# Second layer's heads of a fused three-block model: the split exponentials are transposed by DMA instead of by TensorE

## The chip, the cores and the metric

The kernel runs on one core of one Trainium2 chip, in one launch. The metric is the device time of the whole launch in microseconds, the median of three runs. A change of some 0.5% can be told from none.

## The reference, cut to what matters

The program computes two layers of a first model (a differential and top-k attention layer, then a latent attention layer), and then a second model (a Fourier and windowed attention block with sixteen experts). The change lies in the second layer, the latent attention with 16 heads over 1024 tokens:

```python
def mla_attention(q_nope, q_rope, k_nope, k_rope, v):     # 16 heads, 64 + 32 dims, v 64
    def block(args):                                      # one block of 128 queries
        s = (jnp.einsum('bqhd,bkhd->bhqk', qn, k_nope)
             + jnp.einsum('bqhr,bkr->bhqk', qr, k_rope)).astype(jnp.float32) * scale
        s = jnp.where(chunk_mask(qpos, kpos), s, -jnp.inf)   # causal in chunks of 64
        p = jax.nn.softmax(s, axis=-1)
        return jnp.einsum('bhqk,bkhd->bqhd', p.astype(v.dtype), v)
    ...
def mla_layer(x, ...):
    ...
    o = mla_attention(q_nope, q_rope, k_nope, k_rope, v).reshape(b, s_len, C_WIDTH)
    return x + (o * jax.nn.silu(gate)) @ w_o
```

## The kernel before, in words

Everything is float32 at the interface. A float32 product is made of three TensorE products of high and low parts (`mm3`, L137 to L141). `layer1` (L1034) first projects and stores the latents, then runs a loop over 16 heads (from L1207). A head loads its q and k parts from device memory over SyncE's queue into two-deep buffers (L852, L1212 to L1220), and every fourth head loads v for four heads (L1223).

A head has eight blocks of 128 queries. Since the mask is causal, block qb has qb + 1 blocks of keys. The blocks are packed into five packs, `PACK1` = (7), (6, 0), (5, 1), (4, 2), (3), so a pack has 8, 8, 8, 8 and 4 blocks of 128x128. For each pack (L1229): TensorE makes the scores in PSUM banks (L293), VectorE takes the row maximum and writes masked scores to the SBUF tile `e` (L317, three buffers), VectorE makes the bias `nm` (L1245), ScalarE takes the exponentials in place with their sums (L1247), and `p_to_T` (L331) turns `e` around: TensorE transposes up to four blocks into a PSUM bank `ptp` (L340), ScalarE casts the bank to float16 `pTh` (L341), VectorE subtracts that cast from the bank and writes the rest as float16 `pTl` (L342). `pv_mm` then multiplies with v, three products for each block: `pTh` with both parts of v (L350, L351) and `pTl` with the high part (L352). `norm_o` (L794, the product L801) takes the head's result out, and every second head stores it (L1265).

Between packs the loop runs units of other work: gate products (L783 to L785) in the first eight heads, totals of a modulation vector (L1309 to L1320, each with loads, one small product and a store) from the sixth head on, the second model's bias rows, the output weights (L915 to L919) and halves of the output product (L944 to L949, L1001 to L1011) later. The order of all instructions on each engine, SyncE's queue included, is fixed ahead of the run by a planner that lists the program by its own estimate of each instruction's time. An engine takes its instructions in that order and waits at the head of it. Nearly all loads and stores of this stage go through SyncE's queue.

Two other stages use `p_to_T` too: the first layer's heads (L672, L714) and the second model's windowed attention (L1576).

Of the kernel before, what the change touches and what calls it, by code (L numbers as in the profile page):

```python
# [11 lines left out]
F32 = mybir.dt.float32  # L12
F32R = mybir.dt.float32r
F16 = mybir.dt.float16
# [3 lines left out]
ALU = mybir.AluOpType  # L18
# [4 lines left out]
P = 128  # L23
S = 1024
D = 1024
NT = S // P
# [269 lines left out]
def score_banks(kk, parts, pairs):  # L296


    bs = [kk.bank() for _ in range(0, parts[-1][2], 512)]
    r = []  # L300
    for qb, c0, c1 in parts:
        ps = []
        for b in range(c0 // 512, (c1 - 1) // 512 + 1):
            x0, x1 = max(c0, 512 * b), min(c1, 512 * b + 512)
            sc = bs[b][:, x0 - 512 * b:x1 - 512 * b]
            score_mm(kk, sc, pairs(qb), x0 - c0, x1 - x0)
            ps.append((sc, x0 - c0, x1 - c0))
        r.append(ps)
    return r


def row_max(kk, e, segs, mx):

    last = -3.0e38
    for i, (sc, term, x0, x1) in enumerate(segs):
        m = mx if i == len(segs) - 1 else kk.sm([P, 1], tag="rmx")
        kk.nc.vector.tensor_tensor_reduce(e[:, x0:x1], sc, kk.zeros.to_broadcast([P, x1 - x0]) if term is None else term, scale=1.0, scalar=last,  # L317
                                          op0=ALU.add, op1=ALU.max, accum_out=m)
        last = m


def offsets(pack):

    r, c = [], 0
    for qb in pack:
        r.append((qb, c, c + (qb + 1) * P))
        c += (qb + 1) * P
    return r


def p_to_T(kk, ps, pool, p, nb, cap=NT):  # L331

    nc = kk.nc
    hi = pool.tile([P, cap, P], F16, tag="pT_h", name=kk.nm("pTh"))
    lo = pool.tile([P, cap, P], F16, tag="pT_l", name=kk.nm("pTl"))
    for g in range(0, nb, 4):
        w = min(4, nb - g)
        pt = ps.tile([P, 4, P], F32, tag="tr", name=kk.nm("ptp"))
        for j in range(w):
            nc.tensor.transpose(pt[:, j, :], p[:, (g + j) * P:(g + j + 1) * P], kk.ident)  # L340
        nc.scalar.copy(hi[:, g:g + w, :], pt[:, :w, :])  # L341
        nc.vector.tensor_tensor(lo[:, g:g + w, :], pt[:, :w, :], hi[:, g:g + w, :], op=ALU.subtract)  # L342
    return hi, lo


def pv_mm(kk, out, hi, lo, v1, v2, nb, off=0):

    mm = kk.nc.tensor.matmul
    for j in range(nb):
        mm(out, hi[:, j, :], v1(off + j), start=j == 0, stop=False)  # L350
        mm(out, hi[:, j, :], v2(off + j), start=False, stop=False)  # L351
        mm(out, lo[:, j, :], v1(off + j), start=False, stop=j == nb - 1)  # L352
# [120 lines left out]
def layer0(kk, ps, a, hT, mix_d, gate_d, wo, mod):  # L473
# [145 lines left out]
    for h in range(4):  # L619
# [27 lines left out]
        for i, pack in enumerate(PACK0):  # L647
# [21 lines left out]
            for z, (qb, c0, c1) in enumerate(parts):  # L669
                both = nc.vector.scalar_tensor_tensor(es[0][:, c0:c1], es[1][:, c0:c1], ra[:, z:z + 1], es[0][:, c0:c1],  # L670
                                                      op0=ALU.mult, op1=ALU.add).ins
            hi, lo = p_to_T(kk, ps, pp, es[0], n // P)  # L672
            if i == 0 or at + w > 4:
                pv, at = kk.pv(P), 0
# [119 lines left out]
def norm_o(kk, o, pv, st, vsc):  # L794

    nc = kk.nc
    rs = kk.sm([P, NT], tag="brs")
    nc.vector.reciprocal(rs, st)
    r2 = kk.sm([P, NT], tag="brs2")
    nc.vector.tensor_scalar(r2, rs, vsc[:, 1:2], None, op0=ALU.mult)  # L800
    nc.vector.tensor_tensor(o, pv, r2[:, :, None].to_broadcast([P, NT, 64]), op=ALU.mult)  # L801
# [46 lines left out]
def load_stack(kk, pool, src, row0, tag, lo_first=False, into=None, cols=slice(0, S)):  # L848

    t = pool.tile([P, cols.stop - cols.start], F32R, tag=tag, name=kk.nm(tag), bufs=2) if into is None else into  # L850
    for z in range(2):
        kk.nc.sync.dma_start(t[64 * z:64 * z + 64, :].bitcast(F32), src[z ^ int(lo_first)][row0:row0 + 64, cols])  # L852
    return t
# [180 lines left out]
def layer1(kk, ps, a, hT, hold, mix_d, gate_d, wo, mod, wx):  # L1034

    nc = kk.nc
# [154 lines left out]
    ap_ = ax.enter_context(kk.pool(name="at2", bufs=2))  # L1191
# [15 lines left out]
    for h in range(16):  # L1207
        r0 = 64 * h
        q1 = load_stack(kk, None, qn_d, r0, "q1", into=kp[:, 3 + h % 2, :])
        k1 = kp[:, 5 + h % 2, :]  # L1210
        for z in range(2):
            nc.sync.dma_start(k1[64 * z:64 * z + 64, :].bitcast(F32), kn_d[0][r0:r0 + 64, :])  # L1212
        q2 = ap_.tile([P, S], F32R, tag="q2", name=kk.nm("q2"))
        nc.sync.dma_start(q2[0:64, :].bitcast(F32), qn_d[0][r0:r0 + 64, :])
        for i in range(2):
            for z in range(2):
                b = 64 + 32 * i + 16 * z
                nc.sync.dma_start(q2[b:b + 16, :].bitcast(F32), qr_d[z][i][16 * h:16 * h + 16, :])
        k2 = kp[:, h % 2, :]
        at_ = nc.sync.dma_start(k2[0:64, :].bitcast(F32), kn_d[1][r0:r0 + 64, :]).ins  # L1220
        if h % 4 == 0:
            with kk.tc.issue_after(lk[-1]) if h else ExitStack():
                nc.sync.dma_start(vh[:, :, :, r0:r0 + 256], v_d[:, :, :, r0:r0 + 256])  # L1223
        lk.append(at_)
        if h % 2 == 0:
            o = ap_.tile([P, NT, P], F32, tag="o", name=kk.nm("oc"), bufs=1)
        st = kk.sm([P, NT], tag="bst")
        pv = kk.pv(64)
        for i, pack in enumerate(PACK1):  # L1229
            parts = offsets(pack)  # L1230
            n = parts[-1][2]
            e = ap_.tile([P, S], F32, tag="p", name=kk.nm("e"), bufs=3)
            mx = kk.sm([P, 2], tag="mxc")
            nm = kk.sm([P, 2], tag="nmx")

            def pairs(qb):
                sl = slice(qb * P, (qb + 1) * P)
                return (q1[:, sl], k1), (q2[:, sl], k2), (q2[:, sl], k3)

            rows_ = score_banks(kk, parts, pairs)  # L1240
            for z, (qb, c0, c1) in enumerate(parts):
                d = S - (c1 - c0)
                row_max(kk, e[:, c0:c1], [(sc, hide[:, d + x0:d + x1], x0, x1) for sc, x0, x1 in rows_[z]], mx[:, z:z + 1])
            z = len(pack)
            nc.vector.tensor_scalar(nm[:, 0:z], mx[:, 0:z], -CS, LN_PSC, op0=ALU.mult, op1=ALU.add)  # L1245
            for z, (qb, c0, c1) in enumerate(parts):
                nc.scalar.activation(e[:, c0:c1], e[:, c0:c1], AF.Exp, bias=nm[:, z:z + 1], scale=CS, accum_out=st[:, qb:qb + 1])  # L1247
            hi, lo = p_to_T(kk, ps, ap_, e, n // P)
            for qb, c0, c1 in parts:
                b = slice(c0 // P, c1 // P)  # L1250
                pv_mm(kk, pv[:, qb, :], hi[:, b], lo[:, b], lambda j: vh[:, j, 0, r0:r0 + 64], lambda j: vh[:, j, 1, r0:r0 + 64],
                      qb + 1)
            if h >= 5 and i % 2 == 0:
                mod2.run(1, mp)
            if (h, i) in BIAS1_AT:
                rows.run(1, mp)
            if h < GATES1_HEADS and i in (1, 3):
                gates.run(1)
            if h == GATES1_HEADS and i < 4 or h >= 12 and i == 0:
                prep.run(1)  # L1260
            if (h, i) in HALF1_AT:
                halves.run(1)
        norm_o(kk, o[:, :, (h % 2) * 64:(h % 2) * 64 + 64], pv, st, vsc)
        if h % 2:
            nc.sync.dma_start(mix_d[:, (h // 2) * P:(h // 2 + 1) * P].rearrange("(t p) c -> p t c", p=P), o)  # L1265
        if h == GATES1_HEADS - 1:
            gates.run()
            gx.close()
            lhs_pool = wx.enter_context(kk.pool(name="lhs1", bufs=1, side="right"))
            prep, halves = wo(hx.enter_context(kk.pool(name="wx1", bufs=1, side="right")), lhs_pool)  # L1270
# [602 lines left out]
def tile_model(ctx: ExitStack, tc: tile.TileContext, a: dict, out: bass.AP, part=None):  # L1873
# [61 lines left out]
    bias_d, rows = bias_rows(kk, ps, a["rel_bias_2"], a["c_oh2"], 8, 384, 33, "b2", 8.0, last=-BIG)  # L1935
    wx = ExitStack()
    layer1(kk, ps, a, hT1, hold, mix_d[1], gate_d[1], wo1, (totals, rows), wx)

    def finish_l1(op, hook):
# [229 lines left out]
```

## Time and profile before

| | us |
|---|---|
| runs, median of 3 | 2592.82 |
| lowest, highest | 2587.34, 2599.93 |
| the profiled execution, device time | 2589.32 |
| its span in the profile | 2587.5 |

The page of the profile gives the busy time of each engine over the span and the chain of work that ended last. Engines: PE is TensorE's products, PEld its loading of the stationary operand, DVE VectorE, ACT ScalarE, POOL GpSimd, SPq SyncE's queue of DMA issues. A line such as L340 is that of the kernel, and where a helper serves several stages, the stretch of time tells them apart. The heads of the second layer run from about 1090 to 1462 us of the span.

### The profile page before, as it was taken

The numbers are of one execution on the slowest core, as the hardware profiler recorded it, in microseconds if no ns is written. First come the engines' busy times: TensorE is split into PE (matmuls) and PEld (weight loads), VectorE is DVE, ScalarE is ACT, GpSimd is POOL, SyncE is SP. The second block draws the span as 40 slices with busy tenths as digits, with TensorE's granted clock in tenths as the row PEclk, the third lists the DMA queues.
The fourth block names the chain that finished last, engine by engine and source line by source line (L and its number), as shares of the span: only waits on it lengthen the run. The fifth ranks groups of instructions, "written<-read, shape, count | busy, mean of one in ns | idle before, by whom it ended". The sixth has DMA issues, their size and how long they took to land.

```text
span 2587.5 us, 40940 instructions
## 1 busy us (share of the span) xinstructions
PE 2355.9 (91%) x14412; PEld 1843.1 (71%) x14412; DVE 1797.5 (69%) x4575; ACT 1347.5 (52%) x2635; POOL 438.7 (17%) x626
## 2 busy tenths in 40 slices
PE   7988888898998878999989979989985999999998
PEld 6866666676777866788767768877864777777776
DVE  4459987877986355366776674677666777777775
ACT  4345675455653333255564375355452666666664
POOL 0000147757740013100000000011000101110110
PEclk9999888899999899999999989989997999999999
DMA  4442476566656227854776461545684999999994
GB/s 131 127 135 79 135 204 184 158 188 191 188 154 208 78 99 258 260 147 123 182 192 170 133 204 55 137 111 163 190 302 184 347 382 351 358 363 374 359 353 137
DMA packets 302637, 523.80 MB, mean 202 GB/s; under 512 B 46022, under 2 KB 191582, under 8 KB 302432
## 3 DMA queue, kind: packets, MB, share of 16 engines
q1 hardware_dynamic: 287456, 467.70, 55.5%
q0 software_dynamic: 14976, 53.49, 6.6%
q8 instruction: 114, 1.87, 0.3%
q14 instruction: 91, 0.75, 0.1%
HBM read 405.18 MB, written 115.65 MB: 201 GB/s over the span
## 4 chain that ended last, share of the span: by engine, by line
PE 61%; DMA 15%; DVE 10%; issue 4%; POOL 4%; ACT 4%; SPq 1%; POOLq 0%; DVEq 0%; ACTq 0%
PE sb L139 6%; PE sb L140 6%; PE sb L141 6%; PE sb L293 5%; PE ptp L340 3%; DMA adw<-w_ada 3%; PE w_gate L1815 2%; PE w_down L1815 2%; PE w_up L1815 2%; DVE tkj L397 2%; PE w_gate L139 2%; PE w_gate L141 2%; PE w_up L139 2%; PE w_up L141 2%; PE w_up L140 2%
## 5 line engine op out<-in xcount | busy, mean ns | idle before, releaser
L341 ACT CAST pTh<-ptp 128x512 f16<-128x512 f32 (+2 forms) x316 | 166.1, 557 | 134.8 <-PE ptp L340 129.0
L342 DVE TENSOR_TENSOR pTl<-ptp,pTh 128x512 f16<-128x512 f32 (+2 forms) x316 | 199.9, 648 | 38.1 <-ACT pTh L341 37.4
L1683 DVE TENSOR_TENSOR ring_l<-mraw,ring_h 128x1024 fp32r<-128x1024 f32 x152 | 183.8, 1223 | 33.6 <-ACT ring_h L1682 31.0
L340 PE MATMUL ptp<-ident,e 128*128 128x128 f32 x1184 | 182.2, 284 | 7.6 <-DVE e L670 2.1
L1682 ACT CAST ring_h<-mraw 128x1024 fp32r<-128x1024 f32 x152 | 156.4, 1048 | 59.0 <-PE w_up L141 20.8
L1683 DVE TENSOR_TENSOR ring_l<-xraw,ring_h 128x1024 fp32r<-128x1024 f32 x136 | 164.7, 1223 | 29.4 <-ACT ring_h L1682 27.0
L1682 ACT CAST ring_h<-xraw 128x1024 fp32r<-128x1024 f32 x136 | 140.7, 1049 | 46.2 <-PE w_up L141 19.9
L340 PEld LDWEIGHTS ptp<-ident,e 128*128 128x128 f32 x1184 | 133.4, 144 | 20.2 <-issue 4.0
L1247 ACT ACTIVATE e<-e,nmx 128x1024 f32<-128x1024 f32 (+7 forms) x128 | 98.4, 770 | 74.5 <-DVE nmx L1245 74.3
L352 PEld LDWEIGHTS <-pTl 128*128 128x128 f16 x1184 | 108.5, 99 | 35.6 <-issue 15.0
L350 PEld LDWEIGHTS <-pTh 128*128 128x128 f16 x1184 | 110.2, 100 | 30.9 <-issue 21.4
L1772 POOL DMA_INDIRECT xg<-h_d,idx x16 | 24.0, 1502 | 598.5 <-DVE gate L1775 550.7
L1298 POOL TENSOR_SCALAR adw<-adw,ada_s 128x256 f32<-128x256 f32 x192 | 109.1, 580 | 93.1 <-DMA adw<-w_ada 92.4
L902 ACT ACTIVATE e<-e,nmx 128x1024 f32<-128x1024 f32 (+7 forms) x128 | 98.5, 772 | 42.7 <-DVE nmx L901 23.4
L351 PEld LDWEIGHTS <-pTh 128*128 128x128 f16 x1184 | 110.0, 99 | 3.9 <-issue 3.2
L293 PE MATMUL sb<-hold_l,q 128*128 128x512 f32 (+3 forms) x384 | 104.0, 359 | 2.0 <-DMA q<-qr 2.0
L317 DVE CUSTOM_DVE_ANT_0 e<-sb,hide 128x512 f32<-128x512 f32 (+3 forms) x128 | 74.5, 583 | 37.6 <-PE sb L293 20.8
L139 PE MATMUL pg<-hold_h,wg_h 128*128 128x512 f32 x192 | 85.7, 446 | 16.3 <-DVE gth L135 14.1
L139 PE MATMUL w_down<-ring_h,hTm_h 128*128 128x512 f32 x192 | 91.3, 476 | 0.0
L139 PE MATMUL w_up<-ring_h,xT_h 128*128 128x512 f32 x192 | 90.3, 470 | 0.0
L139 PE MATMUL w_gate<-ring_h,xT_h 128*128 128x512 f32 x192 | 89.1, 464 | 0.0
L1950 POOL DMA_DIRECT2D xb_d<-x x8 | 4.3, 532 | 496.4 <-DVE rsv L148 448.4
(595 smaller groups left out, 7718.9 us busy)
## 6 DMA issues: line engine op xcount, KB each, us to landing
mraw<-w_up SPq DMA_DIRECT2D x35, 1024.0 KB
mraw<-w_gate SPq DMA_DIRECT2D x34, 1024.0 KB
mraw<-w_down SPq DMA_DIRECT2D x33, 1024.0 KB
xraw<-w_down SPq DMA_DIRECT2D x30, 1024.0 KB
xraw<-w_gate SPq DMA_DIRECT2D x30, 1024.0 KB
xraw<-w_up SPq DMA_DIRECT2D x29, 1024.0 KB
adw<-w_ada SPq DMA_DIRECT2D x96, 256.0 KB
xh_d<-hx SPq DMA_DIRECT2D x48, 256.0 KB
```

What stands on the lines that cost most here:

```text
L139: mm(out, a.hi, b.hi, start=start, stop=False)
L140: mm(out, a.hi, b.lo, start=False, stop=False)
L141: mm(out, a.lo, b.hi, start=False, stop=stop)
L293: mm(sc, a, b[:, k0:k0 + n], start=i == 0, stop=i == len(pairs) - 1)
L340: nc.tensor.transpose(pt[:, j, :], p[:, (g + j) * P:(g + j + 1) * P], kk.ident)
L341: nc.scalar.copy(hi[:, g:g + w, :], pt[:, :w, :])
L342: nc.vector.tensor_tensor(lo[:, g:g + w, :], pt[:, :w, :], hi[:, g:g + w, :], op=ALU.subtract)
L350: mm(out, hi[:, j, :], v1(off + j), start=j == 0, stop=False)
L351: mm(out, hi[:, j, :], v2(off + j), start=False, stop=False)
L1682: nc.scalar.copy(w.hi, raw_of(i))
L1683: nc.vector.tensor_tensor(w.lo, raw_of(i), w.hi.bitcast(F32), op=ALU.subtract)
L1815: nc.tensor.matmul(acc[n], xT.full[:, j, :], raw_of(i)[:, j], start=j == 0, stop=False)
```

## The change

The sixteen heads of the second layer call a new function `p_to_T_dma` in place of `p_to_T`. It casts the whole pack of exponentials to float16 on ScalarE while the queries are still on the partitions, and issues a DMA transpose of that cast on SyncE's queue; VectorE subtracts the cast from the exponentials, and a second DMA transpose takes the low part. Both parts lie in one row buffer `pHL`, two deep. The transposed high part has three buffers and the low part two; `e` has two buffers instead of three. The other callers keep `p_to_T`.

```diff
+def p_to_T_dma(kk, pool, p, nb):
+
+    nc = kk.nc
+    n = nb * P
+    hl = pool.tile([P, 2, S], F16, tag="pHL", name=kk.nm("pHL"), bufs=2)
+    hi, lo = [pool.tile([P, NT, P], F16, tag=f"pT_{z}", name=kk.nm("pT" + z), bufs=b) for z, b in (("h", 3), ("l", 2))]
+    nc.scalar.copy(hl[:, 0, :n], p[:, :n])
+    nc.sync.dma_start_transpose(hi[:, 0:nb, :], hl[:, 0, :n])
+    nc.vector.tensor_tensor(hl[:, 1, :n], p[:, :n], hl[:, 0, :n], op=ALU.subtract)
+    nc.sync.dma_start_transpose(lo[:, 0:nb, :], hl[:, 1, :n])
+    return hi, lo
...
-            e = ap_.tile([P, S], F32, tag="p", name=kk.nm("e"), bufs=3)
+            e = ap_.tile([P, S], F32, tag="p", name=kk.nm("e"), bufs=2)
...
-            hi, lo = p_to_T(kk, ps, ap_, e, n // P)
+            hi, lo = p_to_T_dma(kk, ap_, e, n // P)
```

## Rows read from the trace of the kernel before

**Rows 1.** The page: busy time of the engines, and the chain by engine.

```profile
PE 2355.9 (91%) x14412; PEld 1843.1 (71%) x14412; DVE 1797.5 (69%) x4575; ACT 1347.5 (52%) x2635; POOL 438.7 (17%) x626
...
PE 61%; DMA 15%; DVE 10%; issue 4%; POOL 4%; ACT 4%; SPq 1%; POOLq 0%; DVEq 0%; ACTq 0%
```

**Rows 2.** Busy time by stretches; the last three columns are clock, DMA share, rate.

```profile
core 0: us, PE busy (x) PEld busy (x) DVE busy (x) ACT busy (x) POOL busy (x), PEclk, DMA share, GB/s
1000.00:1090.00 90.00, 77.33 (x317) 59.96 (x316) 37.23 (x60) 25.17 (x45) 21.31 (x32) 0.96 0.83 279
1090.00:1137.00 47.00, 47.00 (x434) 39.94 (x433) 30.01 (x91) 28.18 (x62) 0.00 (x0) 1.00 0.48 123
...
1278.00:1325.00 47.00, 37.63 (x397) 29.62 (x396) 36.52 (x104) 28.88 (x60) 0.00 (x0) 0.95 0.77 205
...
1090.00:1462.00 372.00, 351.69 (x3268) 282.91 (x3267) 256.77 (x733) 203.39 (x435) 0.00 (x0) 0.98 0.60 155
```

**Rows 3.** Chain of waits, 1090 to 1462: by line; then pieces (start, us, what).

```profile
by line: PE sb L293 18.2%; PE ptp L340 11.7%; DMA mod_d<-adx 8.5%; DMA adx<-ada_d 6.5%; PE pg L139 6.2%; PE pg L140 6.1%; PE pg L141 6.0%; PE pv L352 3.2%; PE pv L350 3.0%; PE pv L351 2.9%; DMA gtt<-gate_d 2.8%; DMA woraw<-o_w_o 2.6%; PE pm
...
1186.85 0.91 PE ptp L340 x8
...
1248.05 4.21 DMA mod_d<-adx
1252.27 2.14 DMA adx<-ada_d
...
1271.12 6.55 DMA mod_d<-adx
```

**Rows 4.** Groups, 1090 to 1462: count, busy us, mean ns, idle before.

```profile
L342 DVE TENSOR_TENSOR pTl<-ptp,pTh 128x512 f16<-128x512 f32 x140 | 93.4, 682 | 28.4 <-ACT pTh L341 28.2
L340 PE MATMUL ptp<-ident,e 128*128 128x128 f32 x560 | 85.6, 284 | 2.5 <-ACT e L1247 1.9 <-DVE gtt L1011 0.5
L341 ACT CAST pTh<-ptp 128x512 f16<-128x512 f32 x140 | 77.2, 583 | 60.9 <-PE ptp L340 58.3 <-PE pv L352 2.1
```

**Rows 5.** Waits, 1090 to 1462: us in total, times, longest.

```profile
ACT pTh L341 <- PE ptp L340: 58.3, 48, 4.1
...
DVE e L317 <- PE ptp L340: 16.7, 18, 3.7
```

**Rows 6.** DMA queue, 1090 to 1462: packets, MB, share of 16 engines.

```profile
q1 hardware_dynamic: 44414, 57.19, 59.0%
```

**Rows 7.** Busy time by stretches under load, columns as in rows 2.

```profile
1099.00:1108.00 9.00, 9.00 (x113) 7.64 (x112) 5.83 (x20) 5.45 (x13) 0.00 (x0) 1.00 0.89 220
...
2300.00:2500.00 200.00, 200.00 (x831) 141.47 (x830) 154.12 (x217) 127.76 (x173) 19.36 (x10) 1.00 0.98 366
```

**Rows 8.** DMA queue, 1143.2 to 1152, columns as in rows 6.

```profile
q1 hardware_dynamic: 2224, 1.31, 55.2%
```

**Rows 9.** SyncE's queue, 1090 to 1462: start, us of issue, what.

```profile
1098.88 0.45 SPq L852 DMA_DIRECT2D hold_l<-qn_hi  x1
1099.38 0.59 SPq L852 DMA_DIRECT2D hold_l<-qn_lo  x1
...
1132.95 0.60 SPq L1223 DMA_DIRECT2D hold_h<-v_d  x1
...
1213.52 0.22 SPq L1320 DMA_DIRECT2D mod_d<-adx  x1
...
1461.91 0.34 SPq L1309 DMA_DIRECT2D adx<-ada_d  x1
```

**Rows 10.** SyncE's own waits, 1090 to 1462: us in total, times, longest.

```profile
SPq L852 <- PE sb L293: 49.2, 12, 10.0
SPq L220 <- DVE wg_l L135: 37.0, 4, 10.3
```

**Rows 11.** The page: groups out of SBUF with 128x1024 elements, columns as rows 4.

```profile
L1682 ACT CAST ring_h<-xraw 128x1024 fp32r<-128x1024 f32 x136 | 140.7, 1049 | 46.2 <-PE w_up L141 19.9
L1683 DVE TENSOR_TENSOR ring_l<-xraw,ring_h 128x1024 fp32r<-128x1024 f32 x136 | 164.7, 1223 | 29.4 <-ACT ring_h L1682 27.0
```

## What the change will do: the prediction

> **What bounds the kernel now.** I read the page first (engine totals and the chain that ended last), then the trace by stretches, to find the stage that the change touches, and then that stage alone: its chain of waits, its groups of instructions, its DMA queue and SyncE's own waits. Over the whole span TensorE is busy for 91% and carries 61% of the chain [rows 1]. The sixteen heads of the second layer run from about 1090 to 1462 us. That stage is 372 us long; TensorE is busy for 352 us of it, VectorE for 257, ScalarE for 203, and the 16 DMA engines for a share of 0.60 [rows 2]. [...] The chain of the stage says the same: scores (L293) and gate products are last most of the time, the transposes (L340) hold 11.7% of it, and two DMA chains of a filler (mod_d to adx, adx to its product) hold 15.0% [rows 3]. [...]
>
> **What is removed.** One head has packs of 8, 8, 8, 8 and 4 blocks: 36 blocks, 9 evictions. Sixteen heads have 576 TensorE transposes (the stretch holds 560 of them) and 144 casts and 144 subtractions out of PSUM [rows 4]. Eight transposes take 0.91 us of the chain [rows 3], 0.114 us each, so 576 x 0.114 = 65.5 us of TensorE's order; that is the most that can be gained. The least, where nothing replaces them, is what they hold of the chain: 11.7% of 372 = 43.5 us [rows 3]. The waits of ScalarE and VectorE for these transposes (58.3 and 16.7 us) go too [rows 5], but neither engine was last, so I count them at nothing.
>
> **What changes on ScalarE and VectorE.** 144 casts of 0.583 us (84 us) become 64 of 128x1024 and 16 of 128x512; the nearest rows are the ring's casts at 1.049 us, so 64 x 1.049 + 16 x 0.583 = 76 us [rows 4, 11]. 144 subtractions of 0.682 us (98 us) become 64 x 1.223 + 16 x 0.682 = 89 us [rows 4, 11]. Both save some 8 us on engines with 115 us or more to spare [rows 2], so they count as zero. The sources now lie in SBUF and no PSUM bank is held, but the scores' banks are the same as before.
>
> **What is added.** Each of the 80 packs issues two DMA transposes on SyncE's queue: 128 of 262 KB and 32 of 131 KB, together 37.7 MB. The trace of before has no DMA transpose, so I bound each of its three prices.
>
> *Issue.* SyncE issues 262 groups of rows in the stage, 135 us in all (the first and the last stand in rows 9); an ordinary issue takes 0.22 to 0.59 us [rows 9]. 160 x 0.5 = 80 us would give 215 of 372 us: hidden, if a transpose is issued like a load. Against that: every one waits at the head of an in-order queue for its cast or subtraction. Behind it stand the next head's q and k loads, the gate stores and the filler's loads; TensorE's scores and the filler's product wait for those. SyncE waits today as well, up to 10 us at a time for a buffer that the scores free [rows 10], and a transpose planned behind such a wait comes late by as much.
>
> *Landing.* The chain shows 2.14 us for an idle ring and 6.55 us for a busy one [rows 3]. Two slots of the row buffer mean that two packs may be under way: cast 1.05 + subtraction 1.22 + issue 0.5 + landing. With 2.1 to 6.6 us that is 4.9 to 9.4 us for two packs; two packs now take 2 x 372 / 80 = 9.3 us and would take 7.7 us with all 65.5 us gained. So the saving is covered up to a landing of some 4.9 us, and beyond 6.5 us the slots themselves make the stage longer. I cost this at zero in the sum, near its edge.
>
> *DMA engines' time.* The stage needs 0.60 x 372 = 223 us of all 16 engines now [rows 2]; its queue moved 57.2 MB [rows 6]. For 37.7 MB more the best price is the experts' loads, 366 GB/s at a share of 0.98 [rows 7], 373 GB/s: 101 us. The worst row of the stage is 220 GB/s at 0.89 [rows 7], 247 GB/s: 153 us. The nearest in form is the 512-byte packets of the output's store, 1.31 MB in 55.2% of 8.8 us [rows 8], 270 GB/s: 140 us, which I take since a transpose too moves short rows. Sum: 223 + 140 = 363 us of work at a share of 1.0, where TensorE would then need 372 - 65 = 307 to 328 us. The DMA engines become the bound.
>
> [...]
>
> **The sum.** The engines don't reach a share of 1.0 over a stage whose loads come in bursts: the best stretch next to this one has 0.83, and the best of it 0.77 [rows 2]. With 0.83: 363 / 0.83 = 437 us, 65 us more than 372. The profiled execution took 2589.3 us (span 2587.5); the median is 3.5 us above it. 2589.3 + 65 + 3.5 = 2658 us. From (223 + 101) / 0.83 = 390 to (223 + 153) / 0.77 = 488 us, the forecast's own range is +18 to +116: 2611 to 2709 us. A TensorE that waits more also loses clock, 0.05 of it in the worst stretch now [rows 2]; it then has time to spare, so this stays in the range.
>
> **The rivals.** *It is hidden, and the saving stays.* The ring idles between bursts in the first half, TensorE has no gap there, and two packs can be under way. This needs landings below 4.9 us and a price near 373 GB/s: (223 + 101) / 0.98 = 331 us, less than the stage has. It gives -43.5 to -65.5 us, likeliest 2549 us, at best 2527. Against it: a DMA share of 0.60 to 0.77 and a SyncE queue that already ends waits of TensorE. *It cancels:* shares between these two, 2593 us.
>
> *The issue is paid by the block.* If SyncE must push each 128x128 block by itself at the price of a small issue, 0.22 to 0.45 us, then 1152 blocks take 253 to 518 us, and with the 135 us of now SyncE needs 388 to 653 us. The middle, 0.34, gives 392 + 135 = 527 us: +155, 2748 us. It decides from 0.21 us a block, where SyncE's time passes 372 us. For it: a transpose writes its 8 blocks across the order in which it reads them, unlike any DMA of the trace; against it: a load of 1024 KB over 128 partitions takes no longer to issue than one of 256 KB [rows 9]. [...]
>
> *The transposes pass one at a time.* If a transpose doesn't overlap the next, 160 landings follow each other: at 4.2 us, between 2.14 and 6.55 [rows 3], 672 us, +300, 2893 us. From 2.3 us each on, the row of 160 is longer than the stage. For it: all go down one queue, with a rearrangement that no row shows; against it: plain loads overlap freely. [...]
>
> **How the numbers follow.** DMA-bound as summed 0.36, hidden with a gain 0.24, cancelled 0.08, issue by the block 0.20, one at a time 0.12. I predict the likeliest, 2658 us. The range goes from the best case, 2527, to 2900, which leaves out the upper half of the last rival and the tails of the others, some 1 in 10. About 0.5%, 13 us, is what a measurement of this kernel can tell from no change. Faster by more: 0.24. Within: 0.08, and the lowest end of the forecast adds 0.02, so 0.10. Slower: 0.66.
>
> **What would show it.** In the profile after, L340 must be gone from this stage (608 of 1184 left), its casts must read SBUF at about 1.05 us, and the DMA queue must move 37.7 MB more. The forecast is right if the stage's DMA share is over 0.8 and TensorE waits on DMAs of pTh and pTl; SyncE's issue of a transpose should be about 0.5 us. The issue rival shows as a SyncE issue of 2 us or more, the one-at-a-time rival as landings that grow down the queue at a low DMA share. I am wrong if TensorE stays without gaps in the first half and the stage ends early, or if the time moves outside 1090 to 1462 us.

## The result, and the profile after

The changed kernel takes 2696.06 us (median of 4 runs) against 2590.08 us of the kernel before in the same runs: a ratio of 1.041, 95% interval 1.0378 to 1.0442. It is slower by 106 us, inside the predicted range and inside the forecast's own range (2611 to 2709), 38 us above the forecast. The page of the profile after, engine totals and chain, as in [rows 1]:

```profile
PE 2353.5 (87%) x13836; PEld 1815.0 (67%) x13836; DVE 1799.9 (67%) x4511; ACT 1347.7 (50%) x2571; POOL 440.4 (16%) x626
...
PE 54%; DMA 20%; DVE 11%; issue 5%; POOL 4%; ACT 3%; SPq 2%; POOLq 0%; ACTq 0%; DVEq 0%
```

TensorE's share of the chain falls from 61% to 54%, that of DMAs rises from 15% to 20%. Its 576 transposes are gone (13836 instructions, not 14412), but its busy time hardly falls: it now runs at a lower granted clock, and a 128x512 product of the scores (L293, with `q`) took 403 ns in the later heads before and 493 ns after. The stage of the heads shows both (columns as in [rows 2]):

```profile
1278.00:1325.00 47.00, 33.21 (x248) 22.73 (x247) 26.55 (x74) 21.33 (x40) 0.00 (x0) 0.71 0.87 182
...
1090.00:1566.00 476.00, 368.87 (x2769) 271.31 (x2770) 266.85 (x676) 200.49 (x364) 0.00 (x0) 0.83 0.95 206
```

The DMA share is 0.95 (0.60 before), the granted clock 0.83 of full speed (0.98 before). The DMA packets before, 1090 to 1462, and then those of that stretch after, with its queue, columns as in [rows 6]:

```profile
DMA packets 44454, 57.73 MB, mean 155 GB/s; under 512 B 4086, under 2 KB 33022, under 8 KB 44414
...
DMA packets 193192, 98.10 MB, mean 206 GB/s; under 512 B 150197, under 2 KB 180076, under 8 KB 193154
## 3 DMA queue, kind: packets, MB, share of 16 engines
q1 hardware_dynamic: 193154, 97.61, 94.4%
```

Before, 4086 packets of the stage's 44454 were under 512 B; now 150197 are. The 146111 more are, for the 36.4 MB of the 154 transposes in the stretch, some 249 B each: a block of 128x128 float16 moves in pieces about as long as one of its rows, 256 B.

Where in the stage the time went is read from the instruction that takes a head's result out, L801 before and L814 after. It ran for head 0, head 4 and head 15 at these times, before first, then after (start, us, what):

```profile
1115.50 0.68 DVE L801 TENSOR_TENSOR oc<-pv,brs 128x512 f32<-128x512 f32 x1
...
1215.22 0.69 DVE L801 TENSOR_TENSOR oc<-pv,brs 128x512 f32<-128x512 f32 x1 [0.71 <-PE pv L352]
...
1471.21 0.68 DVE L801 TENSOR_TENSOR oc<-pv,brs 128x512 f32<-128x512 f32 x1
```

```profile
1125.48 0.69 DVE L814 TENSOR_TENSOR oc<-pv,brs 128x512 f32<-128x512 f32 x1 [3.77 <-PE pv L365]
...
1225.70 0.69 DVE L814 TENSOR_TENSOR oc<-pv,brs 128x512 f32<-128x512 f32 x1 [1.09 <-PE pv L365]
...
1583.24 0.69 DVE L814 TENSOR_TENSOR oc<-pv,brs 128x512 f32<-128x512 f32 x1 [4.30 <-PE pv L365]
```

Head 0 ends 10 us later: its first masked scores start at 1091.23 instead of 1085.94 us, and the rest is lost inside it. Heads 1 to 4 take 100.2 us where they took 99.7. Heads 5 to 15 take 357.5 us where they took 256.0. Behind head 15 some 7 us come back. So in heads 1 to 4, where TensorE had no gap (before, it was busy for all of the 99.7 us), what its transposes took and the price of the new ones cancel, and 101 us are lost where the loop also runs the filler of the modulation vector and the output weights, whose loads and stores go through SyncE's queue in round trips. The two parts by busy time, first the later heads before, then both parts after:

```profile
1215.20:1471.20 256.00, 235.69 (x2256) 186.07 (x2256) 183.18 (x512) 138.91 (x296) 0.00 (x0) 0.97 0.61 162
```

```profile
1090.00:1225.70 135.70, 120.38 (x976) 95.53 (x977) 82.55 (x211) 67.51 (x123) 0.00 (x0) 0.94 1.02 211
1225.70:1583.20 357.50, 254.86 (x1903) 180.97 (x1902) 190.60 (x483) 139.32 (x254) 0.00 (x0) 0.78 0.90 199
```

The early part has a DMA share of 1.02 (records of packets overlap a little), the late part only 0.90. Now SyncE. The new transposes by their instruction (duration min/median/max in ns, first and last start), and SyncE's queue in the later heads, first and last row of 367 issues:

```profile
L352 ACT CAST pHL<-e x80: 612/1044/1048, 1097.6 to 1577.6; 128x1024 f16<-128x1024 f32 x64, 128x512 f16<-128x512 f32 x16
L353 SPq DMA_TRANSPOSE pTh<-pHL x80: 1189/1251/3782, 1098.7 to 1578.2; - x80
L354 DVE TENSOR_TENSOR pHL<-e,pHL x80: 628/1220/1228, 1098.7 to 1578.2; 128x1024 f16<-128x1024 f32 x64, 128x512 f16<-128x512 f32 x16
L355 SPq DMA_TRANSPOSE pTl<-pHL x80: 1188/1268/5288, 1101.5 to 1579.5; - x80
```

```profile
1225.72 1.25 SPq L355 DMA_TRANSPOSE pTl<-pHL  x1
...
1579.53 1.64 SPq L355 DMA_TRANSPOSE pTl<-pHL  x1
```

An issue takes 1.25 us, not 0.5. Added up over those rows, 109 transposes hold the queue for 156 us and 258 other issues for 120 us: 276 of 357.5 us, 0.77. Before, the later heads' issues held it for 100 of 256 us, 0.39. Heads 1 to 4 hold it even more, 90 of 100.2 us (31 of 99.7 before), and are not longer for it, so a full queue alone doesn't set the loss. Who waits on what, in the stretch 1090 to 1566 (us in total, times, longest):

```profile
ACT e L1260 <- DVE nmx L1258: 148.5, 44, 13.9
...
PEld L363 <- DMA pTh<-pHL: 42.3, 30, 4.3
...
PEld L365 <- DMA pTl<-pHL: 38.5, 35, 2.6
ACT hT_h L931 <- DMA woraw<-o_w_o: 35.6, 7, 21.4
ACT pHL L352 <- DMA pTl<-pHL: 35.0, 22, 3.9
```

Products wait for landings, the cast waits for a row slot, and a load of the output weights that has nothing to do with the change is now waited for up to 21.4 us at a time (4.1 before). The chain of the same stretch by line, to be set beside that of [rows 3]:

```profile
by line: DMA pTl<-pHL 16.8%; PE sb L293 16.2%; PE pg L139 4.4%; issue 4.2%; PE pg L140 4.1%; PE pg L141 4.0%; DMA adx<-ada_d 3.5%; DMA hold_l<-kn_lo 3.2%; DMA pTh<-pHL 3.0%; PE pv L365 2.4%; DMA mod_d<-adx 2.3%; PE poh L139 2.3%; DVE e L317
```

The landing of a DMA is the end of its transfer, and its piece of a chain runs from the start of its issue to there. The landings of the two new transposes hold 19.8% of the 476 us, some 94 us; the TensorE transposes, which held 43.5 us of the stage before, are gone from it. Three causes are in these rows: the DMA engines' time, the waits for landings, and SyncE's queue. The experiments take them apart in part.

### The profile page after: what moved, and what is told of

Read it like the earlier page. It is cut to its first block, busy times and chain, and to the rows that moved or that the text cites. A ratio compares the mean times of both kernels' runs of the same rounds, so it can differ in the third digit from the quotient of the medians.

```text
span 2692.9 us, 40014 instructions
## 1 busy us (share of the span) xinstructions
PE 2353.5 (87%) x13836; PEld 1815.0 (67%) x13836; DVE 1799.9 (67%) x4511; ACT 1347.7 (50%) x2571; POOL 440.4 (16%) x626
## 4 chain that ended last, share of the span: by engine, by line
PE 54%; DMA 20%; DVE 11%; issue 5%; POOL 4%; ACT 3%; SPq 2%; POOLq 0%; ACTq 0%; DVEq 0%
PE sb L139 6%; PE sb L140 6%; PE sb L141 5%; PE sb L293 4%; DMA adw<-w_ada 4%; DMA pTl<-pHL 3%; PE w_gate L1828 2%; PE w_down L1828 2%; PE w_up L1828 2%; DVE tkj L410 2%; PE w_up L139 2%; PE w_gate L139 2%; PE w_up L141 2%; PE w_gate L141 2%; PE w_gate L140 2%
## 5 line engine op out<-in xcount | busy, mean ns | idle before, releaser
L363 PEld LDWEIGHTS <-pTh 128*128 128x128 f16 x1184 | 114.8, 103 | 72.7 <-DMA pTh<-pHL 48.7
L293 PE MATMUL sb<-hold_l,q 128*128 128x512 f32 (+3 forms) x384 | 114.9, 400 | 15.1 <-DMA hold_l<-kn_lo 8.9
L354 DVE TENSOR_TENSOR pHL<-e,pHL 128x1024 f16<-128x1024 f32 (+1 forms) x80 | 88.7, 1113 | 47.8 <-ACT pHL L352 47.4
L341 ACT CAST pTh<-ptp 128x512 f16<-128x512 f32 (+2 forms) x172 | 87.0, 533 | 66.0 <-PE ptp L340 59.7
L364 PEld LDWEIGHTS <-pTh 128*128 128x128 f16 x1184 | 115.4, 103 | 3.2 <-issue 2.8
L342 DVE TENSOR_TENSOR pTl<-ptp,pTh 128x512 f16<-128x512 f32 (+2 forms) x172 | 104.0, 619 | 10.0 <-ACT pTh L341 9.8
L363 PE MATMUL pv<-hold_h,pTh 128*128 128x64 f16 x576 | 74.4, 207 | 37.3 <-DMA pTh<-pHL 37.0
L293 PEld LDWEIGHTS sb<-hold_l,q 128*128 128x128 f32 x384 | 78.6, 222 | 30.9 <-issue 20.7
L365 PE MATMUL pv<-hold_h,pTl 128*128 128x64 f16 x576 | 69.7, 207 | 32.3 <-DMA pTl<-pHL 32.1
L352 ACT CAST pHL<-e 128x1024 f16<-128x1024 f32 (+1 forms) x80 | 75.9, 957 | 40.6 <-DMA pTl<-pHL 37.4
## 6 DMA issues: line engine op xcount, KB each, us to landing
adw<-w_ada SPq DMA_DIRECT2D x96, 256.0 KB
xh_d<-hx SPq DMA_DIRECT2D x48, 256.0 KB
```

What stands on the lines that cost most here:

```text
L293: mm(sc, a, b[:, k0:k0 + n], start=i == 0, stop=i == len(pairs) - 1)
```

## The experiments

**All the transposes added, no product waits.** The kernel before with its TensorE transposes, and the DMA transposes on top, into scratch.

```diff
             hi, lo = p_to_T(kk, ps, ap_, e, n // P)
+            for z in range(2):
+                dump = ap_.tile([P, NT, P], mybir.dt.int16, tag="dump", name=kk.nm("dump"), bufs=3)
+                nc.sync.dma_start_transpose(dump[:, 0:n // P, :], e.bitcast(mybir.dt.int16)[:, z * n:z * n + n])
```

> The kernel before, whole, with 160 DMA transposes of the same shapes added on SyncE's queue. They read the exponentials' own bytes as 16-bit integers and write to three scratch tiles that nobody reads, so no product waits for a landing and TensorE keeps its transposes. Theory (the DMA engines' time is the bound): the stage of the heads had 0.60 of 372 us = 223 us of DMA time; after it has 0.95 of some 490 = 465, so the transposes cost some 225 to 240 us, and they cost that here too: the stage grows to 460 to 490 us and the launch to 2675 to 2710 us, with a DMA share near 0.95. Rival (the wait of the products for a landing, through two slots, is what costs): without such a wait the launch stays within 2590 to 2615 us, and the DMA share is below 0.9.

It took 2692.74 us (2 runs, ratio 1.0391, 1.0343 to 1.0439), as long as the kernel after. The stage, columns as in [rows 2]:

```profile
1090.00:1566.00 476.00, 398.22 (x3286) 309.43 (x3285) 263.23 (x724) 196.21 (x416) 0.00 (x0) 0.92 0.96 205
```

The same DMA share, with a granted clock of 0.92 instead of 0.83. So the transposes as such, on their queue, are enough for the whole loss; neither the products' wait for them nor a clock as low as 0.83 is needed. It doesn't yet say whether bytes or issues do it, and it is not free of waits for landings: VectorE writes a buffer of `e` again only when its added transposes have landed. It waits 42.9 us for that, and these landings are the largest item of the stage's chain, some 57 us:

```profile
by line: DMA dump<-e 11.9%; PE sb L293 11.6%; PE ptp L340 6.7%; DMA adx<-ada_d 6.0%; SPq L1251 5.2%; issue 4.7%; DVE e L317 3.9%; PE pg L139 3.7%; PE pg L141 3.7%; PE pg L140 3.5%; PE poh L139 2.9%; DVE pTl L342 2.7%; PE poh L141 2.6%; PE p
```

**The same bytes as copies.** The two lines above with an ordinary copy in place of the transpose.

> As the kernel with added transposes, but each of the 160 is an ordinary copy of the same bytes (2 KB rows) into the same scratch tiles. Theory (a transpose's price is that of its 256-byte pieces): the copies cost 101 to 140 us of DMA time, so 324 to 363 us of the stage's 372: 2590 to 2620 us, far less than with transposes. Rival (the issues and their waits in SyncE's in-order queue cost, whatever is moved): as long as with transposes, within 15 us.

2621.14 us (2 runs, ratio 1.0115, 1.0086 to 1.0143): +31, a microsecond above what the theory gave and far below the rival. The copies' issue, and the later heads:

```profile
L1251 SPq DMA_DIRECT2D dump<-e x160: 464/473/1630, 1096.6 to 1503.5; - x160
```

```profile
1224.40:1509.00 284.60, 244.78 (x2247) 190.49 (x2246) 186.15 (x515) 138.67 (x295) 0.00 (x0) 0.94 0.82 238
```

Transposes cost 72 us more than copies of the same bytes. Their packets or their issues, 0.47 us here and 1.27 there, can make that.

**The prices alone.** A launch with nothing but four groups of 64 DMAs inside SBUF.

> The model's work is left out; the launch holds only four groups of 64 DMAs inside SBUF on SyncE's queue, each group after the last: transposes of 128x1024 two-byte elements (262 KB), copies of the same bytes in 2 KB rows, copies in 256-byte pieces, transposes of one 128x128 block (33 KB). The 229 to 256 us that the 144 whole transposes' worth took in the stage is 1.6 to 1.8 us of all 16 engines for each. Theory (the price is the transposes' own small pieces): the group's time x DMA share is 64 x 1.6 = 100 us or more, and the copies in 256-byte pieces cost about the same, while those in 2 KB rows take 45 to 62 us. Rival (in the stage the transposes were only slowed by the other loads): alone they cost 270 GB/s or better, under 64 us of DMA time. Rival (the transposition itself is dear, not the pieces): 256-byte copies cost under 0.7 of the transposes. If a transpose were paid by the block at issue, one block would issue in an eighth of the 1.25 us; I expect 1 us or more.

Windows inside the four groups: transposes of 128x1024, copies in 2 KB rows, copies in 256-byte pieces, transposes of one block (the last two columns are DMA share and GB/s):

```profile
5.00:85.00 80.00, 0.00 (x0) 0.00 (x0) 1.00 1.00 191
95.00:135.00 40.00, 0.00 (x0) 0.00 (x0) 1.00 1.02 382
145.00:210.00 65.00, 0.00 (x0) 0.00 (x0) 1.00 0.97 216
225.00:295.00 70.00, 0.00 (x0) 0.00 (x0) 1.00 0.13 26
```

SyncE's queue, the first and the last group (start, us for 64 issues):

```profile
1.95 88.11 SPq L1884 DMA_TRANSPOSE transpose<-src  x64
...
217.93 81.60 SPq L1890 DMA_TRANSPOSE transpose<-src_rows  x64
```

A whole transpose takes 262 KB / 191 GB/s = 1.37 us of all 16 engines, so 37.7 MB take 197 us. In the stretch of the kernel after the same can be estimated: 0.95 x 476 = 452 us in all, less some 61 MB of other traffic at the 3.9 us per MB of before (223 us for 57.2 MB), 239 us, leaves 213 us for some 36.4 MB (154 of the 160), 5.9 us per MB, 221 us for all. By this estimate they are a little dearer in the stage, beside the loads, than alone. Copies in 256-byte pieces run at 216 GB/s, near the transposes and not near the 382 of 2 KB rows: the same bytes in such pieces take nine tenths of the transposes' time (191 / 216 = 0.88). Both rivals on the engines' price fall. And a transpose of one block takes 81.60 / 64 = 1.27 us to issue, near a whole one's 88.11 / 64 = 1.38 us: the price is by the instruction.

**A seventh of the bytes, all of the issues.** As the first experiment, but each added transpose has one block.

```diff
-                nc.sync.dma_start_transpose(dump[:, 0:n // P, :], e.bitcast(mybir.dt.int16)[:, z * n:z * n + n])
+                nc.sync.dma_start_transpose(dump[:, 0, :], e.bitcast(mybir.dt.int16)[:, z * n:z * n + P])
```

> The kernel before with 160 DMA transposes added that nobody reads, as in the first experiment, but each of one 128x128 block (33 KB) only: 5.2 MB in place of 37.7. Alone, such a transpose takes SyncE 1.27 us to issue, the same as a whole one, at a DMA share of 0.13. Theory (the bytes' time on the DMA engines made the loss): 5.2 MB cost some 30 us of DMA time, 250 of 372: 2590 to 2615 us. Rival (SyncE's queue: 160 issues of 1.27 us, each waiting in order for its exponentials, hold up the loads): most of the +103 of the whole ones stays, over 2650 us.

2667.98 us (4 runs, ratio 1.0291, 1.026 to 1.0322): +76 of the +103. The time is the rival's; my theory that the bytes make most of the loss was wrong. The stage and the issue:

```profile
1090.00:1550.00 460.00, 393.99 (x3379) 311.71 (x3378) 270.14 (x749) 204.09 (x436) 0.00 (x0) 0.92 0.55 145
```

```profile
L1251 SPq DMA_TRANSPOSE dump<-e x160: 1093/1176/2331, 1093.8 to 1553.1; - x160
```

The DMA share is 0.55, below that of the kernel before, and the stage is long all the same. SyncE's queue is held for some 0.8 of the later heads here, added up like above. So 160 small transposes cost most of the loss with the engines half idle. Two things in them can do it: issues of 1.2 us in an in-order queue, each of which can also wait for its exponentials, and the landings that VectorE waits for before it writes `e` again. The chain of the stage, then that wait (us in total, times, longest) here and, second, with the copies from 1090 to 1500:

```profile
by line: PE sb L293 11.5%; DMA dump<-e 10.1%; PE ptp L340 7.9%; DVE e L317 5.8%; issue 5.4%; DVE pTl L342 3.3%; ACT e L1247 3.3%; PE pg L139 3.2%; PE pg L141 3.2%; PE pg L140 3.1%; DMA adx<-ada_d 3.0%; DMA mod_d<-adx 2.7%; DMA hold_l<-kn_lo
...
DVE e L317 <- DMA dump<-e: 21.6, 11, 5.7
```

```profile
DVE e L317 <- DMA dump<-e: 24.0, 12, 5.1
```

VectorE waits as long with the copies, which move seven times the bytes and cost 45 us less. So this wait doesn't make the difference between the two; the price of an issue does, as far as is shown, though the planner's order differs as well. How the +76 itself divides is open: the landings' pieces, each with its own issue in it, hold 10.1% of this chain, some 46 us.

**On ScalarE's queue.** `nc.scalar.dma_start_transpose` for both in the kernel after.

> The kernel after with both transposes issued on ScalarE's queue instead of SyncE's. Theory (DMA engines' time): nothing changes on the 16 engines: 2680 to 2720 us, DMA share in the stage again about 0.95. Rival (SyncE's in-order queue, where a transpose takes 1.25 us to issue and holds up loads): SyncE is freed of 200 us of issues and the launch falls by 40 us or more, under 2655 us.

2764.11 us (ratio 1.0654, 1.0623 to 1.0684), slower still. Its queues from 1090 to 1640, and the issue:

```profile
q1 hardware_dynamic: 47138, 60.94, 49.1%
q10 hardware_dynamic: 145600, 36.05, 46.5%
```

```profile
L353 ACTq DMA_TRANSPOSE pTh<-pHL x80: 1204/1254/6626, 1095.8 to 1651.8; - x80
```

This frees SyncE but doesn't test it cleanly, as I had meant: the same 1.25 us and the waits now stand on ScalarE between the exponentials, and the recorded time of the engines' packets, for about the same bytes, grew to 526 us (95.6% of 550) from 452; why isn't shown. The rival's 2655 us failed. I read it as: the issues have no cheap place, not as evidence against SyncE's queue; no run tests that reading.

**Fewer transposes.** Packs 1 and 3 of each head by DMA, the others by TensorE:

```diff
-            hi, lo = p_to_T_dma(kk, ap_, e, n // P)
+            hi, lo = p_to_T_dma(kk, ap_, e, n // P) if i in (1, 3) else p_to_T(kk, ps, ap_, e, n // P, bufs=(3, 2))
```

> The kernel after, but only packs 1 and 3 of each head (16 of its 36 blocks) go by DMA; the others are transposed by TensorE as before. Theory (DMA engines' time): 223 + 16/36 x 230 = 325 us of DMA time, 0.87 of the stage of before, and TensorE is relieved of 29 us: between 2570 and 2610 us. Rival (waits for landings): the cost falls only with the number of packs that wait, 32 of 80, so 0.4 x 106 = +42: about 2632 us.

2627.13 us (ratio 1.0119, 1.0076 to 1.0162): +37, above the theory's 2570 to 2610 and near the 2632 of the rival, the waits for landings. Then the high part alone, without the products with the low part:

```diff
-    nc.vector.tensor_tensor(hl[:, 1, :n], p[:, :n], hl[:, 0, :n], op=ALU.subtract)
-    nc.sync.dma_start_transpose(lo[:, 0:nb, :], hl[:, 1, :n])
...
```

> The kernel after without the low part: no subtraction, no second transpose and no product with the low part, so p is rounded to float16 and the output is a little less exact. Theory (the load on the DMA engines): 223 + 115 = 338 us of DMA time, as with packs 1 and 3 alone and with the added copies, which took +31 and +37: 2610 to 2632 us. Rival (each pack's wait for its landing): all 80 packs still wait for one landing after the cast: over 2650 us. Rival (TensorE): it is relieved of 65 + 17 us, and if the load no longer matters below 0.9 of the engines, the launch falls under 2560 us.

2610.76 us (ratio 1.0065, 1.0041 to 1.0089): +18, at the lower end of the theory's range. All 80 packs still wait for a landing, so the number of waits alone doesn't set the loss. But the run is also without the subtractions and a third of the products with v, and the landings of `pTh` hold 19.5% of its chain from 1090 to 1480, so it doesn't clear the landings. And packs 1 and 3 in the first five heads alone (`if h < 5 and i in (1, 3)`):

> Packs 1 and 3 by DMA in the first five heads only, where TensorE has no gap and SyncE's queue is idle between the heads' loads. With packs 1 and 3 in all heads, heads 1 to 3 took 74.1 us against 77.9 before, 1.3 us a head less. Theory (DMA is dear only where its engines and round trips are loaded): 5 x 1.3 = 6 us gained, 2580 to 2592 us, hardly to be told from before. Rival (any transpose on the queue costs, by bytes): 5/16 of +37 = +12, 2600 us or more.

2612.15 us (ratio 1.0074, 1.0047 to 1.0102): a miss, in the rival's range. Its heads 5 to 15, which hold no transpose, took 277 us instead of 256. What they share with the kernel after is a size that I had not priced: two buffers of `e` instead of three.

**The exponentials' third buffer.** The kernel before with `bufs=2` for `e`, nothing else:

> The kernel before with one size changed: the exponentials' tile e has two buffers instead of three, as in the kernel after; nothing goes by DMA transpose. With transposes in heads 0 to 4 alone, the heads 5 to 15, which hold no transpose, took 277 us against 256 before. Theory (the third e buffer let a pack's maxima run ahead of the round trips on the queue): heads 5 to 15 lose about 20 us here too, the launch takes 2603 to 2618 us. Rival (those heads lost it to another order of the planner, or to what the first heads left behind): within 2585 to 2598 us.

2610.87 us (11 runs, ratio 1.0049, 1.0032 to 1.0066): +13, and heads 5 to 15 take 276 us here too. The same first five heads with three buffers of `e` and one row slot:

> Packs 1 and 3 of the first five heads by DMA, with three e buffers and one row slot. Theory (the missing e buffer cost the heads 5 to 15 their 20 us): these heads take about 256 us again and the launch 2584 to 2598 us, hardly to be told from before. Rival (the transposes of the first heads cost it): 2605 us or more again.

2599.74 us against 2597.86 (ratio 1.0008, 0.9993 to 1.0023): the loss is gone, and heads 5 to 15 take 256.8 us. The ten packs in those five heads by DMA are then neither gain nor loss. Packs 1 and 3 of all heads with three buffers and one row slot:

> Packs 1 and 3 of all heads by DMA as before, but with three e buffers; the room comes from the row buffer pHL, which has one slot instead of two. Theory (a third or more of the +37 was the missing e buffer): 2600 to 2615 us. Rival (the load on the DMA engines alone gave the +37): 2618 to 2640 us, or more, since a single row slot holds up the next cast.

2621.33 us (ratio 1.0086, 1.0064 to 1.0108), +23, in the rival's range. Its interval overlaps that with two buffers, so by the time of the launch the buffer's part is not settled. In the trace heads 5 to 15 take 260.9 us, where they took 289.3 with two buffers; this execution lost its time elsewhere, 13 us up to the end of head 0 and 18 us behind head 15. Last, the whole change with three buffers of `e`, paid for by slots of the rows and of the transposed high part:

```diff
-    hl = pool.tile([P, 2, S], F16, tag="pHL", name=kk.nm("pHL"), bufs=2)
-    hi, lo = [pool.tile([P, NT, P], F16, tag=f"pT_{z}", name=kk.nm("pT" + z), bufs=b) for z, b in (("h", 3), ("l", 2))]
...
+    rh = pool.tile([P, S], F16, tag="pRh", name=kk.nm("pRh"), bufs=2)
+    rl = pool.tile([P, S], F16, tag="pRl", name=kk.nm("pRl"), bufs=1)
+    hi, lo = [pool.tile([P, NT, P], F16, tag=f"pT_{z}", name=kk.nm("pT" + z), bufs=b) for z, b in (("h", 2), ("l", 2))]
...
```

> The kernel after with three e buffers; the room comes from one row slot less for the low part and one slot less for the transposed high part. Theory (at a DMA share of 0.95 the engines' time is the bound, whatever the slots): 2680 to 2710 us. Rival (the missing e buffer is a part of the +106 as well): 2660 to 2680 us.

2734.04 us (ratio 1.0509, 1.0482 to 1.0535), worse by some 30 us and outside both expectations. Its stage and the new longest wait of VectorE:

```profile
1090.00:1600.00 510.00, 373.56 (x2774) 273.74 (x2772) 268.62 (x678) 204.53 (x371) 0.00 (x0) 0.82 0.90 193
```

```profile
DVE pRl L355 <- DMA pTl<-pRl: 105.4, 51, 4.7
```

With one slot for the low rows the subtraction waits 51 times for a landing, and the DMA share falls from 0.95 to 0.90. So "whatever the slots" was wrong. The transposed high part has a buffer less here too, so how much the one row slot costs by itself isn't shown.

None of these kernels beats the kernel before.

## Why the prediction was right or wrong, point by point

*The removal and the work on ScalarE and VectorE.* Right: L340 has left the stage, the cast has a median of 1.044 us and the subtraction 1.220 us, as taken from [rows 11].

*The DMA engines' time.* Two of the three signs came, a DMA share over 0.8 and TensorE waiting for `pTh` and `pTl`; the third, an issue of 0.5 us, didn't. Two sizes were off. The term of 140 us is 197 us alone and an estimated 221 us in the stage; it lies above the upper bound of 153 us, which came from a stretch of larger packets (1.97 MB in 705 of them, 2.8 KB each, from 1099 to 1108). The share that the engines reach was put at 0.83 and is 0.95. With the price alone and the measured share the sum has (223 + 197) / 0.95 = 442 us; with that price and the forecast's share it would have 506. The forecast had 437, so it is luck that the two errors nearly cancel. And a high share is not what most of the loss needs: the stage with one block a transpose is 460 us long at 0.55.

*The issue* is the step that failed most plainly. "160 x 0.5 = 80 us, hidden, if a transpose is issued like a load" is 160 x 1.25 us or more, 235 us over the rows of the stage; it isn't issued like a load. I had named what it does (in-order queue, loads behind it, TensorE's scores and the filler waiting) and priced it at zero. With a seventh of the bytes the transposes cost +76 us, 45 us more than copies with a short issue and all the bytes. The rival that would have caught it was priced by the block, and the price is by the instruction: alone 1.27 us for one block and 1.38 us for eight.

*The landing*, "at zero, near its edge", wasn't at zero: landings of the new transposes hold some 94 us of the stage's chain. The products' wait isn't needed for a loss of this size, as the first experiment shows, but that run isn't without a wait for landings: `e` waits for them, some 57 us of the chain. With one slot of the low rows, and one buffer of the high part less, the loss is +136.

*The third buffer of* `e` I didn't price at all. Taken away alone it costs 13 us. The first experiment keeps it and loses as much as the change, so the parts don't simply add.

*The rivals.* Hidden with a gain: heads 1 to 4, where TensorE was relieved, gain nothing at a DMA share of 1.02 up to the end of head 4 and a SyncE queue held for 0.9 of them. One at a time: 64 whole transposes take 88 us alone, 1.38 us each, against 3.4 us from an issue to its landing (the median of that group), so they overlap.

*The forecast, 2658 us, was near for a reason that is half of the truth.* Bytes at a cheap issue cost +31 (copies), few bytes at a dear issue +76, both +103. That these add up may be chance: packets of copies and transposes differ, and a planner lists each kernel anew. Shown is that 160 transposes on SyncE's queue make a loss of this size, and that most of it stays when they are small. How the loss of the kernel after divides between the engines' time, the landings and SyncE's queue is left open; so is how much of the queue's cost is the planner's order, which I didn't try to change.

## What to carry to other kernels

Before a step moves to a DMA queue, price three things apart: the engines' time by packets of the size that the step really makes (here 216 GB/s in pieces of 256 B, 382 in rows of 2 KB), the issuing engine's time for each instruction (here 1.25 us a transpose, 0.47 a copy), and what stands behind it in that in-order queue (here a load waited for up to 21.4 us at a time, 4.1 before). The same step came out even in heads where it relieved a TensorE without gaps, and cost 101 us in heads whose filler makes round trips through the same queue, so read the two parts apart. A buffer taken away to make room is part of the change and wants its own line in the sum (here +13 us alone).

## What the runs showed of the hardware that was not expected

A DMA transpose inside SBUF on SyncE's queue takes 1.2 to 1.4 us to issue, for 33 KB as for 262 KB, where a copy of 262 KB takes 0.47 us. With nothing beside them, those of 262 KB move 191 GB/s, half of the 382 GB/s of copies in 2 KB rows; plain copies in 256-byte pieces inside SBUF reach 216 GB/s. With the transposes on ScalarE's queue beside the loads on SyncE's, the recorded time of about the same bytes on the engines was 526 us against 452; why isn't shown.
